# Squares of the output projection issued as tasks, and the last 256 tokens written token by token

## The chip, the cores and the metric

The kernel runs on one core of one Trainium2 chip. The metric is the device time of one execution in microseconds (us); the number of a kernel is the median of its runs.

## The reference

The program is one step of a two-layer network (DEPTH 2, width D_MODEL 2048) on 128 context tokens and 512 latent tokens, 640 in all. Each layer normalises its input, runs two mixers beside each other (attention and gated linear attention in layer 0, neighbourhood attention and a gated MLP in layer 1), multiplies by a gate and projects back to 2048 features. The change touches only what surrounds the two projections back and the final norm:

```python
def rms_norm(x, g, eps=1e-6):
    xf = x.astype(jnp.float32)
    y = xf * lax.rsqrt(jnp.mean(xf * xf, axis=-1, keepdims=True) + eps)
    return (y * g.astype(jnp.float32)).astype(x.dtype)
...
for l in range(DEPTH):
    shift, scale, gate = modulation(c_ctx, ada_w[l], ada_b[l])
    h = rms_norm(x, norm_g[l]) * (1.0 + scale) + shift
    ...
    x = x + gate * (y @ w_out[l])
y_prompt = rms_norm(x, final_norm_g)
```

For the latent tokens the same is done with their own modulation. So after each projection the squares of x have to be summed over the 2048 features of each token, once for the norm of layer 1 and once for the final norm.

## The kernel before

**Layout.** Activations lie with features on the 128 partitions and tokens along the free axis: a strip is 128 features by 640 tokens, and 16 strips make a token's 2048 features. Context tokens are columns 0 to 127, latent tokens 128 to 639.

**Products.** Weights and activations are single precision, each split into a high and a low part: `whi` and `wlo` for weights, `acth` and `actl` for activations. One product is three matrix instructions: `acth` by `whi`, `actl` by `whi`, `acth` by `wlo` (all at line 397). ACT makes a high part by copying into the shorter format; POOL makes a weight's low part by subtracting it (`wlo<-wraw,whi`, or `wlo<-rs,whi` for sums of two weight tiles, in line 214, through which every ACT, DVE and POOL instruction passes). So ahead of each group of products there is a weight load on SP, a row of ACT and a row of POOL.

**Order.** There is no order by hand. A planner in the program (`Pace`) keeps a model of when each engine will be free. The products set its time; between them `tick` calls issue weight splits (`wpump`) and give a turn to tasks, which are Python generators put on a list with `spawn`. A task goes on when the flags that it names are set (`wait`), when the model says that its operand is ready (`until`) and when the engines that it names are not booked further ahead than so many us (`calm`). A step that the main program needs can be forced with `need`, which gives turns to the tasks until the flag is there. What is issued on one engine is run in that order. All DMAs that this text speaks of go out on SP's queue (`dma`, line 431), but for the last transfers, of which every other one goes out on ACT's (line 2684).

**The projections back.** `out_proj(l)` runs over 16 output strips, for layer 1 in the order of their features, for layer 0 in the order OUT0. The first two are computed together by `kpair`, the next twelve two by two by `spair`, which shares sums of weight tiles (a scheme of Strassen's kind), and the last two by `kpair` in layer 0 and by `hpair` in layer 1. `hpair` computes columns 0 to 383 (CUT) of both strips first and then columns 384 to 639, so that the first part can be finished while the second is computed. `spair` overwrites halves of `acth` and `actl`; the kept copies lie in DRAM (`bh_dram`, `bl_dram`) and `unfold` (line 1130) brings them back for the last pair, one copy at each turn of the task.

**Evacuation.** `out_evac` (line 1969) makes, for each strip, a function that takes the product out of its bank: y = G·product + x, on DVE, into one of eight slots of Y (NY = 8). In the same call it has the squares summed: `ssq_add` (line 1240) lets ACT write y² into a buffer and POOL add it to `ssq`:

```python
        def square(y, c):
            if l == 1 and f == KT - 1:
                nc.scalar.activation(self.sq[:, : c.stop - c.start], y[:, c], AF.Square)
            else:
                self.ssq_add(self.ssq, y, f, self.sq if self.cut == CUT else self.sqs.next(), c)
```

For the first fourteen strips this happens in two halves of 320 columns; in the profile these rows are `arena<-Y 128x320` on ACT and `arena<-arena 128x320` on POOL. The buffers are a ring of two (`sqs`). The last two strips of layer 0 had their squares in a task of their own (`squares`) already. The strips of y go to DRAM too (`spill`): in layer 1 the first eight, since Y has only eight slots, and `reload` (line 2638) fetches them again when the copies of `unfold` are in, into free parts of rs, arena and adas. `handover` with its task `rewrite` (line 994) turns the strips of layer 0 into the `acth` and `actl` of layer 1.

**The end.** `final(half)` (line 2646) runs twice, for columns 0 to 383 and 384 to 639. A product with a matrix of ones sums `ssq` over the partitions, so that every partition holds the sum of each token; `rms` makes the root of its inverse by Ln and Exp on ACT and one step of Newton's on DVE, on rows as wide as the half. Then each of 16 strips is multiplied by the final gain g (a value for each partition) and by the token's root (a row), on DVE, or on POOL for the five strips of POOLED, where ACT has multiplied by g ahead of time. Two strips go out with each DMA, as runs of 1.5 KB in the first half and 1 KB in the second.

Of the kernel before, what the change touches and what calls it, by code (L numbers as in the profile page):

```python
# [14 lines left out]
ALU = mybir.AluOpType  # L15
# [224 lines left out]
class Trunk:  # L240
# [601 lines left out]

    def hpair(self, c1, c2, after):

        self.cut = CUT
        for half, order in enumerate(((AGAIN, KEPT), (KEPT, AGAIN))):
            if half:
                self.quiet, self.hold = True, 6.0
            p = {}
            for end in range(2):  # L850
                for c in (c1, c2):
                    if not end:
                        if half == 0 and self.chunks[c][3]:
# [140 lines left out]
    def handover(self, ready, free, used, order, at, src, loads, spare, cs, shift=None):  # L994
# [26 lines left out]

        def rewrite():
            if shift is not None:
                yield from self.wait("shift1")
            for k in order:
                yield from self.wait(f"{free}:{k}", f"in:{k}", *(f"evac{c}" for c in cs if k in (6, 7)))
                x = tile_(k)
                yield from self.until(x)
                while (w := self.pace.ready("a", [self.pace.span(x)], []) - self.now) > 0:
                    yield w  # L1030
                yield from self.calm(self.calms[0], "ag")
                if shift is not None:
# [12 lines left out]
                yield  # L1045
# [923 lines left out]
    def out_evac(self, l, n, f, xsrc, spill):  # L1969
        nc = self.nc  # L1970
        box = {}

        def square(y, c):
            if l == 1 and f == KT - 1:
                nc.scalar.activation(self.sq[:, : c.stop - c.start], y[:, c], AF.Square)
            else:
                self.ssq_add(self.ssq, y, f, self.sq if self.cut == CUT else self.sqs.next(), c)

        def squares(y):
            if n == KT - 1:  # L1980
                yield from self.wait("squares")
            for q, s in ((slice(0, HT), self.sqs.next()), (slice(HT, T), self.sqs.next())):
                yield from self.wait("x1:14")
                yield from self.calm(2.0, "a")
                nc.scalar.activation(s, y[:, q], AF.Square)
                yield from self.until(s)
                yield from self.calm(4.0, "v")
                nc.vector.tensor_tensor(self.ssq[:, q], self.ssq[:, q], s, ALU.add)
                yield
            self.flags.add("squares")  # L1990

        def evac(pa, pb):
            G, at = self.G[l], self.cut
            y = self.Y[:, n % NY, :]
            if pa is not None:
                if n < NY:
                    self.clear(f"Y{n}", "C", "R")
                x = box["x"]
# [25 lines left out]
        return pre, evac  # L2024
# [144 lines left out]
    def program(self):  # L2169
# [473 lines left out]
        self.flags.add("reload")  # L2643
        yield

    def final(self, half):
        nc, d, L = self.nc, self.d, self.L
        c = slice(CUT, T) if half else slice(0, CUT)
        n = c.stop - c.start
        t, u = (m[:, :n] for m in L["ms"])  # L2650
        if half:
            yield from self.wait("prescaled")
        p = self.sm()[:, :n]
# [3 lines left out]
        yield from self.until(self.sq[:, :n])  # L2657
        self.mm(p, self.ones, self.sq[:, :n], start=False)
        if not half:
            yield 0.8  # L2660
        self.rms(r, p, t)
        q = self.sm()[:, :n]
        nc.vector.scalar_tensor_tensor(q, t, 1.5, r, ALU.add, ALU.mult)
        if half:
            nc.scalar.activation(u, t, AF.Copy, bias=1.5)
            nc.gpsimd.tensor_tensor(u, u, r, ALU.mult)
            self.flush()
        else:
            nc.scalar.activation(u, q, AF.Copy)
            self.flags.add("fr")  # L2670
            yield from self.wait("reload")
        at = 0
        for k in range(KT):
            y, g = self.x2(k)[:, 0, c], self.fg[:, k : k + 1]
            if k in self.POOLED:
                if not half:
                    yield from self.calm(1.5, "a")
                    nc.scalar.activation(self.x2(k), self.x2(k), AF.Copy, scale=g)
# [3 lines left out]
            if half and (k % 2 or k == 0):  # L2682
                eng = (nc.sync, self.tc.nc.scalar)[(k + 1) // 2 % 2]
                eng.dma_start(d["o_y"][:, at : k + 1, c], self.x2(at, k + 1 - at)[:, :, c])
                at = k + 1
            elif k % 2 and not half:
                self.dma(d["o_y"][:, k - 1 : k + 1, c], self.x2(k - 1, 2)[:, :, c])
            if not half:
                if k == self.POOLED[-1]:
                    self.flags.add("prescaled")  # L2690
                yield 0.3
        self.flags.add(f"final{half}")
        yield


class Ring:
# [9 lines left out]


_OUTS = {
    "o_y": [128, KT, T],
    "o_ak": [2, 128, 128],  # L2710
    "o_av": [2, 128, 128],
    "o_state": [2, 4, 128, 256],
# [109 lines left out]


def _result(r):
    y = r["o_y"].transpose(2, 1, 0).reshape(T, D)
# [32 lines left out]
```

## Time and profile before

| | before |
|---|---|
| median of 3 runs | 2104.3 us (2100.51, 2104.3, 2105.4) |
| profiled execution, whole | 2104.64 us |
| its span, first to last instruction | 2102.8 us |
| mean granted TensorE clock | 0.996 |
| busy: TensorE | 98% |
| busy: DVE / ACT / POOL | 62% / 51% / 62% |
| bytes moved | 340.18 MB |

A row of a timeline reads: start, duration, engine, line, operation, output<-inputs, shapes, count, and in brackets how long the engine stood idle before it and what ended that. A row of groups reads: line, engine, operation, names and shapes, count | busy us, mean ns of one | idle time before them and what ended most of it. A row of a window reads: stretch, its length, busy us (instructions) of PE, PEld, DVE, ACT and POOL, then the granted TensorE clock, the busy share of the DMA engines and GB/s. PE is TensorE, PEld its weight loads, SPq the queue of SP. Line numbers are those of the kernel before.

### The profile page before, as it was taken

Reading aid. Unit: us, or ns where it says so; the run is one execution under the profiler, and the core shown is the slowest. Engines: PE = TensorE matmul, PEld = TensorE weight load, DVE = VectorE, ACT = ScalarE, POOL = GpSimd, SP = SyncE. Lnnn points to the kernel's source line nnn. Section 1 sums busy time; section 2 is a strip of 40 time slices with the busy share of each in tenths; the row PEclk is TensorE's granted clock in tenths of the full one; section 3 lists DMA queues with packets and bytes.
Section 4 is the critical chain, followed back from the end, with each engine's and each line's share of the span. In section 5 each row is a group of like instructions: output and inputs, shape, how many; then the busy total and the mean of one; then the engine's idle time right before and its main releaser. Section 6 shows DMA issues by size and latency. Waiting matters only on the chain.

```text
span 2102.8 us, 40256 instructions
## 1 busy us (share of the span) xinstructions
PE 2052.0 (98%) x14345; PEld 2000.7 (95%) x14345; DVE 1305.9 (62%) x3034; ACT 1078.3 (51%) x2485; POOL 1301.4 (62%) x1090
## 2 busy tenths in 40 slices
PE   7999999999999999999999999999999999999997
PEld 6899999999999999999999999999999999999996
DVE  4746586676465664787376878787454444466434
ACT  5645565554566866543564434444444544454443
POOL 4656565355455563888755656555655577767884
PEclk9999999999999999999999999999999999999998
DMA  9966343335465544565634454444222344363426
GB/s 362 389 218 207 120 140 123 116 116 175 149 200 173 171 162 149 175 211 181 227 126 129 131 167 152 137 149 148 97 75 94 105 134 131 120 224 116 139 93 240
DMA packets 192841, 340.18 MB, mean 162 GB/s; under 512 B 20896, under 2 KB 70144, under 8 KB 192640
## 3 DMA queue, kind: packets, MB, share of 16 engines
q1 hardware_dynamic: 191296, 336.45, 48.4%
q8 instruction: 112, 1.84, 0.4%
q10 hardware_dynamic: 1344, 1.17, 0.2%
q14 instruction: 89, 0.73, 0.1%
HBM read 303.03 MB, written 31.88 MB: 159 GB/s over the span
## 4 chain that ended last, share of the span: by engine, by line
PE 79%; DMA 7%; DVE 6%; POOL 3%; issue 3%; ACT 2%; SPq 1%; ACTq 0%; POOLq 0%; DVEq 0%
PE bank L397 76%; POOL wlo L214 2%; PE bank L402 2%; DVE arena L214 1%; DVE adas L214 1%; DVE Y L214 1%; DMA adas<-gateT 1%; DMA more<-ada 1%; DVE bank L214 1%; ACT arena L214 1%; DMA Y<-xT 1%; DMA adas<-ada 1%; SPq L431 1%; PE bank L1426 1%; POOL actl L214 0%
## 5 line engine op out<-in xcount | busy, mean ns | idle before, releaser
L397 PE MATMUL bank<-acth,whi 128*128 128x320 f32 (+3 forms) x3320 | 1020.9, 318 | 7.3 <-ACT bc L214 3.0
L397 PE MATMUL bank<-acth,wlo 128*128 128x320 f32 (+3 forms) x3320 | 993.9, 310 | 3.2 <-POOL wlo L214 3.0
L397 PE MATMUL bank<-actl,whi 128*128 128x320 f32 (+3 forms) x3320 | 993.2, 310 | 1.1 <-DMA actl<-bl_dram 1.1
L214 POOL TENSOR_TENSOR wlo<-wraw,whi 128x512 fp32r<-128x512 f32 (+1 forms) x446 | 564.5, 1278 | 388.9 <-ACT whi L214 302.3
L397 PEld LDWEIGHTS bank<-acth,whi 128*128 128x128 f32 (+1 forms) x3320 | 617.1, 189 | 16.2 <-ACT bc L214 4.4
L397 PEld LDWEIGHTS bank<-acth,wlo 128*128 128x128 f32 (+1 forms) x3320 | 617.2, 189 | 4.7 <-POOL wlo L214 4.7
L397 PEld LDWEIGHTS bank<-actl,whi 128*128 128x128 f32 (+1 forms) x3320 | 617.2, 189 | 3.2 <-DMA actl<-bl_dram 1.6
L214 POOL TENSOR_TENSOR wlo<-rs,whi 128x384 fp32r<-128x384 f32 x370 | 409.2, 1125 | 190.8 <-ACT whi L214 154.3
L214 ACT ACTIVATE whi<-wraw 128x512 fp32r<-128x512 f32 (+1 forms) x456 | 260.7, 587 | 93.0 <-PE bank L397 66.4
L214 ACT ACTIVATE whi<-rs 128x384 fp32r<-128x384 f32 x370 | 183.3, 517 | 59.4 <-PE bank L397 51.2
L397 PE MATMUL bank<-eh,wlo 128*128 128x322 f32 (+1 forms) x666 | 206.8, 311 | 2.2 <-POOL wlo L214 2.2
L397 PE MATMUL bank<-eh,whi 128*128 128x322 f32 (+1 forms) x666 | 209.0, 314 | 0.0
L397 PE MATMUL bank<-el,whi 128*128 128x322 f32 (+1 forms) x666 | 206.8, 310 | 0.0
L214 DVE TENSOR_TENSOR wraw<-rs 128x768 f32<-128x768 f32 x74 | 99.1, 1339 | 131.6 <-DMA rs<-w_odd 46.6
L214 POOL TENSOR_TENSOR prod<-adas,mixrow 128x512 f32<-128x512 f32 x94 | 123.6, 1324 | 84.4 <-ACT prod L214 59.1
L214 DVE CUSTOM_DVE_ANT_0 adas<-adas,bank,partg 128x256 bf16<-128x256 f32 (+1 forms) x290 | 156.2, 539 | 12.0 <-DMA adas<-ada_g 4.6
L214 ACT ACTIVATE arena<-arena,bc 128x512 f32<-128x512 f32 (+4 forms) x189 | 97.8, 538 | 76.4 <-DVE arena L214 71.3
L397 PEld LDWEIGHTS bank<-eh,wlo 128*128 128x128 f32 x666 | 125.5, 188 | 3.5 <-POOL wlo L214 3.5
L397 PEld LDWEIGHTS bank<-el,whi 128*128 128x128 f32 x666 | 125.8, 189 | 0.0
L397 PEld LDWEIGHTS bank<-eh,whi 128*128 128x128 f32 x666 | 125.5, 188 | 0.1
L214 DVE TENSOR_TENSOR bank<-bank,sums 128x320 f32<-128x320 f32 (+1 forms) x148 | 70.7, 493 | 72.8 <-PE bank L397 56.3
L214 DVE CUSTOM_DVE_ANT_0 adas<-adas,bank,part 128x512 bf16<-128x512 f32 x142 | 105.6, 744 | 9.5 <-DMA adas<-ada 6.9
(221 smaller groups left out, 2467.7 us busy)
## 6 DMA issues: line engine op xcount, KB each, us to landing
wraw<-w_even SPq DMA_DIRECT2D x176, 256.0 KB, 3.4
adas<-ada_g SPq DMA_DIRECT2D x128, 256.0 KB, 3.6
adas<-ada SPq DMA_DIRECT2D x128, 256.0 KB, 3.6
rs<-w_odd SPq DMA_DIRECT2D x50, 384.0 KB, 3.2
wraw<-w_odd SPq DMA_DIRECT2D x74, 256.0 KB, 3.6
wraw<-w_out SPq DMA_DIRECT2D x60, 256.0 KB, 3.5
rs<-w_odd SPq DMA_DIRECT2D x50, 256.0 KB, 3.9
Y<-ada SPq DMA_DIRECT2D x24, 512.0 KB, 7.7
```

What stands on the lines that cost most here:

```text
L214: return f(*args, **kw)
L397: self.nc.tensor.matmul(out, lhsT, rhs, start=start, stop=stop, **kw)
L402: self.nc.tensor.transpose(out, in_, self.ident[:k, :k])
L431: self.nc.sync.dma_start(out, in_)
L1426: nc.tensor.matmul(o, c, w, start=j < 4, stop=j >= 12)
```

## The change

Three things are changed.

1. *Squares.* For the first fourteen strips of both projections `square` no longer issues anything; it spawns a task `late` for each half. The task waits for the task before it, for y, until ACT is booked no more than 1.0 us ahead for the square, and until POOL is booked no more than 1.5 us ahead for the addition, and then sets a flag `sq{l}:{i}`. Three places now ask for such a flag: an evacuation of strip 8 and later (the squares of the strip whose slot it overwrites), the evacuations of the last pair in layer 1, and `rewrite`.
2. *Final gain ahead of time.* `prescale` and `scale` multiply columns 384 to 639 of each strip by g in place, on whichever of ACT, DVE and POOL the planner holds free first; the last two strips get it in a row of DVE behind their evacuation (`ends2`).
3. *The last 256 tokens.* `final` now does columns 0 to 383 only. `last` does the rest with tokens on the partitions: 32 transposes of 128x128 by TensorE bring the scaled strips into eight banks, six products with two columns of ones sum the squares for each token into one column, the root is made on 4 columns, and each bank is copied out to SBUF by ACT or DVE in turn with the root as a value for each partition. Eight transfers on SP write them to a new output `o_z` [256 tokens, 2048], six of them in runs of 2 KB. The host puts both outputs together.

```diff
@@ hpair @@
-        self.cut = CUT
+        self.cut, self.ends2 = CUT, []
...
-            self.spawn(after(half), first=True)
+            self.hb = list(p.values())
+            self.spawn(after() if half else self.final(), first=True)
@@ handover, rewrite @@
-                yield from self.wait("shift1")
+                yield from self.wait("shift1", f"sq0:{2 * KT - 5}")
@@ out_evac @@
         def square(y, c):
-            if l == 1 and f == KT - 1:
+            if n < KT - 2:
+                self.spawn(late(y, c, 2 * n + (c.start > 0)))
+            elif l == 1 and f == KT - 1:
                 nc.scalar.activation(self.sq[:, : c.stop - c.start], y[:, c], AF.Square)
+            elif l == 1 and f == KT - 2 and c.start == CUT:
+                nc.scalar.activation(self.sqs.list[0][:, : T - CUT], y[:, c], AF.Square)
...
+        def late(y, c, i):
+            yield from self.wait("ssq" if i == 0 else f"sq{l}:{i - 1}")
+            yield from self.until(y[:, c])
+            yield from self.calm(1.0, "a")
+            if i < 2:
+                nc.scalar.activation(self.ssq[:, c], y[:, c], AF.Square)
+            else:
+                s = self.sqs.next()
+                nc.scalar.activation(s, y[:, c], AF.Square)
+                yield from self.until(s)
+                yield from self.calm(1.5, "g")
+                nc.gpsimd.tensor_tensor(self.ssq[:, c], self.ssq[:, c], s, ALU.add)
+            self.flags.add(f"sq{l}:{i}")
+            yield
...
+            if at == CUT:
+                self.need(f"sq1:{2 * KT - 5}")
...
+                else:
+                    self.need(f"sq{l}:{2 * (n - NY) + 1}")
...
+                if at == CUT:
+                    nc.vector.tensor_scalar(x[:, at:T], y[:, at:T], self.fg[:, f : f + 1], None, ALU.mult)
+                    self.ends2.append(x[:, at:T])
@@ program @@
-        do(lambda: self.spawn(self.reload()))
+        do(lambda: [self.spawn(x) for x in (self.reload(), self.prescale())])
-        pair("h", self.final)
+        pair("h", self.last)
@@ new: scale, prescale, last @@
+    def scale(self, k):
...
+        if e == "a":
+            nc.scalar.activation(x, x, AF.Copy, scale=g)
+        else:
+            (nc.vector if e == "v" else nc.gpsimd).tensor_scalar(x, x, g, None, ALU.mult)
...
+    def last(self):
...
+        def put(g):
+            for j in range(4):
+                x = rows[4 * (g // 2) + j][:, 128 * (g % 2) : 128 * (g % 2) + 128]
+                self.tr(bank[g][:, 128 * j : 128 * j + 128], x)
...
+        for i in range(2):
+            for j, x in enumerate(parts):
+                self.mm(p[:, 2 * i : 2 * i + 2], x[:, 128 * i : 128 * i + 128], self.ones[:, 0:2], start=j == 0, stop=j == 2)
...
+        self.rms(r, p, t)
+        nc.vector.scalar_tensor_tensor(r, t, 1.5, r, ALU.add, ALU.mult)
+        put(6)
+        for g, (b, o) in enumerate(zip(bank, outs)):
+            if g == 5:
+                yield from self.wait("final0")
+                put(7)
...
+            if i:
+                nc.vector.tensor_scalar(o, x, r[:, 2 * i : 2 * i + 1], None, ALU.mult)
+            else:
+                nc.scalar.activation(o, x, AF.Copy, scale=r[:, 2 * i : 2 * i + 1])
+            z = d["o_z"][128 * i : 128 * i + 128, 512 * k : 512 * k + 512]
+            nc.sync.dma_start(z if len(o.shape) == 2 else z.rearrange("p (a b) -> p a b", b=T - CUT), o)
```

How this moves instructions is seen in the order of each engine. First POOL, behind the evacuation of the first pair of strips in layer 1's projection, as it was before (`wlo` are low parts of weights, `arena<-arena` an addition of squares):

```order
L214 TENSOR_TENSOR wlo<-rs_8159,whi 128x384
L214 TENSOR_TENSOR arena_8164<-arena_8164 128x320 x2
L214 TENSOR_TENSOR wlo<-rs_8159,whi 128x384
L214 TENSOR_TENSOR wlo<-wraw,whi 128x384 x2
L214 TENSOR_TENSOR wlo<-rs_8159,whi 128x384 x2
L214 TENSOR_TENSOR arena_8164<-arena_8164 128x320
L214 TENSOR_TENSOR wlo<-rs_8159,whi 128x384 x2
```

The same place of POOL now:

```order
L214 TENSOR_TENSOR wlo<-rs_8159,whi 128x384 x2
L214 TENSOR_TENSOR wlo<-wraw,whi 128x384 x2
L214 TENSOR_TENSOR wlo<-rs_8159,whi 128x384 x4
L214 TENSOR_TENSOR wlo<-wraw,whi 128x512
L214 TENSOR_TENSOR wlo<-wraw,whi 128x384 x2
L214 TENSOR_TENSOR wlo<-rs_8159,whi 128x384 x3
L214 TENSOR_TENSOR arena_8164<-arena_8164 128x320
```

The three additions that stood between these low parts come behind them.

Then SP's queue in the last pair of layer 1, before (`acth<-bh_dram` and `actl<-bl_dram` are the copies of `unfold`, `wraw<-w_out` are weight loads):

```order
L431 DMA wraw<-w_out 128x512
L431 DMA acth<-bh_dram 128x320
L431 DMA wraw<-w_out 128x512
L431 DMA actl<-bl_dram 128x320
L431 DMA acth<-bh_dram 128x320
L431 DMA wraw<-w_out 128x512
L431 DMA actl<-bl_dram 128x320
L431 DMA wraw<-w_out 128x512
```

and now:

```order
L431 DMA wraw<-w_out 128x512
L431 DMA actl<-bl_dram 128x320
L431 DMA acth<-bh_dram 128x320
L431 DMA wraw<-w_out 128x512
L431 DMA actl<-bl_dram 128x320
L431 DMA acth<-bh_dram 128x320
L431 DMA wraw<-w_out 128x512
L431 DMA actl<-bl_dram 128x320
```

The last copy stood ahead of the last load of this piece and now stands behind it.

Last, TensorE behind its last product of weights. Before, only a sum by ones followed it:

```order
L397 MATMUL bank_68<-acth,whi 128x256
L397 MATMUL bank_68<-actl,whi 128x256
L397 MATMUL bank_68<-acth,wlo 128x256
L397 MATMUL bank_73<-arena_8164,ones 128x256 x2
```

Now (the six products with 128x2 are the sums for each token, `ident` marks transposes):

```order
L397 MATMUL bank_69<-acth,wlo 128x256
L402 MATMUL bank_67<-ident,rs_8159 128x128 x4
L402 MATMUL bank_68<-ident,rs_8159 128x128 x4
L402 MATMUL bank_70<-ident,arena_8164 128x128 x2
L402 MATMUL bank_70<-ident,adas 128x128 x2
L397 MATMUL bank_74<-ones,arena_8164 128x2 x6
L402 MATMUL bank_73<-ident,arena_8164 128x128 x2
L402 MATMUL bank_73<-ident,adas 128x128 x2
L402 MATMUL bank_71<-ident,Y 128x128 x4
L402 MATMUL bank_69<-ident,Y 128x128 x4
```

Three banks are filled ahead of the sums and the others behind them; two more banks follow with the same kinds of rows.

More of the change, by code (lines that the diff above doesn't have):

```diff
@@ L2644, in reload, with prescale, final @@
         yield
-    def final(self, half):
-        nc, d, L = self.nc, self.d, self.L
[L2648 to L2653, printed above, removed]
+    def scale(self, k):
+        if k >= KT - 2 or f"sc{k}" in self.flags:
+            return
+        nc, t = self.nc, self.pace.t
+        x, g = self.x2(k)[:, 0, CUT:T], self.fg[:, k : k + 1]
+        yield from self.until(x)
+        while f"sc{k}" not in self.flags:
+            w, e = min((max(t[e], self.now) + w, e) for e, w in (("a", 0.4), ("v", 0.4), ("g", 0.8)))
+            if w < self.now + 1.5:
+                break
+            yield w - self.now - 1.4
+        else:
+            return
+        if e == "a":
+            nc.scalar.activation(x, x, AF.Copy, scale=g)
+        else:
+            (nc.vector if e == "v" else nc.gpsimd).tensor_scalar(x, x, g, None, ALU.mult)
+        self.flags.add(f"sc{k}")
+    def prescale(self):
+        yield from self.wait(f"sq1:{2 * KT - 5}")
+        for k in (*range(NY, KT - 2), *range(NY)):
+            if k == 0:
+                yield from self.wait("reload")
+            yield from self.scale(k)
+            yield
+        self.flags.add("scaled")
+        yield
+    def final(self):
+        nc, d, L = self.nc, self.d, self.L
+        c = slice(0, CUT)
+        t, u = (m[:, :CUT] for m in L["ms"])
+        p = self.sm()[:, :CUT]
         r = self.rstd[:, c]
@@ L2656, in final @@
         self.mm(p, self.ones, self.ssq[:, c], stop=False)
[L2657 to L2660, printed above, removed]
+        yield from self.until(self.sq)
+        self.mm(p, self.ones, self.sq, start=False)
+        yield 0.8
         self.rms(r, p, t)
-        q = self.sm()[:, :n]
+        self.qb = self.sm()
+        q = self.qb[:, :CUT]
         nc.vector.scalar_tensor_tensor(q, t, 1.5, r, ALU.add, ALU.mult)
[L2664 to L2672, printed above, removed]
+        nc.scalar.activation(u, q, AF.Copy)
+        yield from self.wait("reload")
         for k in range(KT):
             y, g = self.x2(k)[:, 0, c], self.fg[:, k : k + 1]
+            yield from self.scale(k)
             if k in self.POOLED:
-                if not half:
-                    yield from self.calm(1.5, "a")
-                    nc.scalar.activation(self.x2(k), self.x2(k), AF.Copy, scale=g)
+                yield from self.calm(1.5, "a")
+                nc.scalar.activation(y, y, AF.Copy, scale=g)
                 nc.gpsimd.tensor_tensor(y, y, u, ALU.mult)
@@ L2681, in final @@
                 nc.vector.scalar_tensor_tensor(y, y, g, q, ALU.mult, ALU.mult)
[L2682 to L2691, printed above, removed]
@@ L2708 @@
 _OUTS = {
-    "o_y": [128, KT, T],
+    "o_y": [128, KT, CUT],
+    "o_z": [T - CUT, D],
     "o_ak": [2, 128, 128],
@@ L2824, in _result @@
 def _result(r):
-    y = r["o_y"].transpose(2, 1, 0).reshape(T, D)
+    y = np.concatenate([r["o_y"].transpose(2, 1, 0).reshape(CUT, D), r["o_z"]], 0)
     heads = lambda t: np.ascontiguousarray(t.transpose(2, 0, 1))[None, None]
```

32 lines of the change are left out of this document (31 added, 1 removed).

## The prediction

> **What bounds the kernel now.** I read the page first, then who waited for whom, then the timeline at the waits and behind the last matrix product. From the page:
>
> ```profile
> span 2102.8 us, 40256 instructions
> PE 2052.0 (98%) x14345; PEld 2000.7 (95%) x14345; DVE 1305.9 (62%) x3034; ACT 1078.3 (51%) x2485; POOL 1301.4 (62%) x1090
> ```
>
> TensorE is busy for 98% of the span, and the change takes nothing off its products. So it can gain only where TensorE waits, and behind its last product. The list of TensorE's waits, for the whole run and then for 870 to 980, 1890 to 1930 and 2040 to 2080 us (total, times, longest):
>
> ```profile
> PE bank L397 <- POOL wlo L214: 5.2, 7, 1.1
> PE bank L397 <- POOL wlo L214: 3.7, 5, 1.0
> PE bank L397 <- POOL wlo L214: 1.1, 1, 1.1
> PE bank L397 <- DMA actl<-bl_dram: 1.1, 2, 0.6
> ```
>
> Six of the seven waits for a weight's low part (wlo) lie in the first strips of the two output projections, 3.7 us in layer 0 and 1.1 us in layer 1: 4.8 us. The seventh (0.4 us, the rest of 5.2) is in the last pair. What holds POOL there is shown by the timeline at 955 to 972 us and at 1914 us (the last row is a window behind them, with the busy time of PE, PEld, DVE, ACT and POOL):
>
> ```profile
> 960.69 0.99 ACT L214 ACTIVATE arena<-Y 128x320 f32<-128x320 f32 x2 [6.07 <-DVE Y L214]
> 961.24 2.44 POOL L214 TENSOR_TENSOR arena<-arena 128x320 f32<-128x320 f32 x2 [4.76 <-ACT arena L214]
> 963.64 2.68 POOL L214 TENSOR_TENSOR wlo<-wraw,whi 128x384 fp32r<-128x384 f32 x2
> 1914.72 1.02 POOL L214 TENSOR_TENSOR arena<-arena 128x320 f32<-128x320 f32 x1 [0.89 <-ACT arena L214]
> ...
> 1920.00:1940.00 20.00, 20.00 (x138) 20.00 (x137) 9.22 (x13) 8.84 (x20) 18.57 (x17) 1.00 0.47 156
> ```
>
> ACT stands 6.07 us before a square (arena<-Y) because its operand Y is not there; POOL stands 4.76 us before the addition of that square. Each engine takes its instructions in order, so the low parts that TensorE waits for stand behind them. The engines are not full; the order holds them.
>
> Behind the last product (it starts at 2087.51 and lasts 0.28) come 15.0 us. The first window shows the DMA engines nearly empty, the next ones full:
>
> ```profile
> 2087.51 0.28 PE L397 MATMUL bank<-acth,wlo 128*128 128x256 f32 x1
> ...
> 2088.00:2090.00 2.00, 1.40 (x4) 0.59 (x4) 1.36 (x3) 1.93 (x5) 2.00 (x3) 1.00 0.17 62
> 2090.00:2093.00 3.00, 0.00 (x0) 0.00 (x0) 2.09 (x5) 1.16 (x3) 1.67 (x3) 0.85 1.00 360
> 2093.00:2095.00 2.00, 0.00 (x0) 0.00 (x0) 2.00 (x6) 0.00 (x0) 1.92 (x4) 0.50 0.61 211
> 2095.00:2100.00 5.00, 0.00 (x0) 0.00 (x0) 2.20 (x6) 0.00 (x0) 1.63 (x3) 0.50 1.03 341
> 2101.00:2102.80 1.80, 0.00 (x0) 0.00 (x0) 0.00 (x0) 0.00 (x0) 0.00 (x0) 0.50 0.15 54
> ...
> 2084.59 0.37 SPq L431 DMA_DIRECT2D o_y<-arena  x1
> 2089.15 2.28 SPq L431 DMA_DIRECT2D o_y<-Y  x3
> 2097.47 1.09 SPq L431 DMA_DIRECT2D o_y<-Y  x1
> ```
>
> (The last two numbers of a window are the DMA engines' busy share and GB/s; SPq rows are SP issuing a transfer, 0.37 us at its quickest and 0.76 in the crowded three.) Between 2090 and 2101.3 the engines are at their limit except for 0.8 us of room at 2093 to 2095. The tail is a chain of instructions up to about 2092 and a queue of bytes after it.
>
> **The change, part by part.**
>
> *Squares as tasks.* The same number of squares and additions, so no engine gains or loses work; what moves is their place. In the new order of POOL in layer 1 the three additions that stood ahead of the strip's low parts come after all of them, so that wait goes: 1.1 us. In layer 0 the low parts of the sum (wlo<-wraw) pass two additions of 2.44 us together, more than the longest wait of 1.0 us there; the later ones still have one square or two between them. Bounds: all 4.8 us go, or none (POOL's additions of 1.0 us each land ahead of a later low part that is just as urgent). I take 3.0 of 3.7 us in layer 0, since the freed place is longer than each wait, and all of layer 1: **-4.1 us**. The new waits of the evacuation for squares of eight strips ago and of the rewriting for the last square of layer 0 only order the program; the squares they name stand ahead of them by then, and I cost them at nothing. Their cover is the eight strips in between and, for the rewriting, the last pair of strips; with it gone the price is one late addition, 1.0 us.
>
> *The fetch of the kept halves.* In the last pair each copy back (acth<-bh, actl<-bl) now stands behind one more weight load on SP. The last of them decides:
>
> ```profile
> 2065.40 0.32 SPq L431 DMA_DIRECT2D actl<-bl_dram  x1
> 2065.90 0.33 SPq L431 DMA_DIRECT2D wraw<-w_out  x1
> ...
> 2069.61 0.45 PE L397 MATMUL bank<-actl,whi 128*128 128x384 f32 x1 [0.64 <-DMA actl<-bl_dram]
> ```
>
> The two change places. The load waits for a slot (it went at 2065.90), so the copy goes at about 2066.0 in place of 2065.40, lands 0.6 us later, and TensorE has that wait on top. From its issue to the product that waited for it went 4.2 us (2069.61 less 2065.40). Bounds: 0, if it travels less crowded there, and 1.1, if the copies come to cost TensorE twice what they cost it now. I take most of the delay of the issue: **+0.5 us.**
>
> *The scaling by the final gain ahead of time.* Fourteen strips of 128x256 on ACT, DVE and POOL, most of them while POOL has nothing to do:
>
> ```profile
> 2082.61 1.02 POOL L214 TENSOR_TENSOR rs<-rs,arena 128x384 f32<-128x384 f32 x1 [9.88 <-ACT rs L214]
> L214 POOL TENSOR_TENSOR Y<-Y,arena 128x256 f32<-128x256 f32 x3 | 2.1, 727 | 0.0
> ```
>
> Six on POOL at 0.73 us (two operands; one operand is not shown at this size) are 4.4 us in 9.9 us of idle time; even at double that they fit. One more scaling on ACT comes before the table load, some 0.4 us on the first 384 tokens, which are not last. Nothing on the path; without that cover 4.4 us.
>
> *The tail.* It removes eleven DVE rows and five POOL rows of 256 tokens and the row-wide root; it adds 32 transposes, six small products, a root on 4 columns and eight evictions of 128x512.
>
> ```profile
> L402 PE MATMUL bank<-ident,Y 128*128 128x128 f32 x108 | 20.6, 273 | 0.5 <-DVE Y L214 0.5
> L397 PE MATMUL bank<-small,adas 128*128 128x2 f32 x48 | 7.7, 230 | 3.9 <-ACT adas L214 3.0 <-DVE adas L214 0.9
> L214 ACT ACTIVATE bc<-bank 128x2 f32<-128x2 f32 x90 | 15.3, 170 | 155.3 <-DVE arena L214 148.8 <-DVE YB L214 4.4 <-DVE Y L214 1.4
> L214 ACT ACTIVATE Y<-bank 128x512 f32<-128x512 f32 x37 | 22.1, 598 | 52.4 <-PE bank L397 41.5 <-PE bank L402 10.3
> L214 DVE TENSOR_SCALAR arena<-bank 128x320 f32<-128x320 f32 x8 | 3.9, 492 | 5.0 <-PE bank L397 4.8
> L214 DVE SCALAR_TENSOR_TENSOR Y<-Y,small,bank 128x384 f32<-128x384 f32 x5 | 2.9, 604 | 0.0
> L214 DVE SCALAR_TENSOR_TENSOR el<-part,eh 128x4 fp32r<-128x4 f32 x2 | 0.2, 158 | 0.0
> ```
>
> From the last product's end, 2087.8, on DVE: the last evacuation to 2088.3 (0.5), one scaling to 2088.6, the four rows of the first 384 tokens that stand ahead (4 x 0.60) to 2091.0. TensorE needs 12 x 0.19 = 2.3 us for transposes (20.6 over 108) and 6 x 0.16 = 1.0 us for the sums, to 2091.1, beside it. ACT's two small rows at 0.17 end at 2091.4 and DVE's three at 2091.9. Then ACT evicts four banks at 0.60 and DVE four at 0.79 (0.49 for 320 columns, and 512 at the same pace), the last at 2095.1. SP issues eight transfers from 2092.5 on; at 0.37 us each it is ruled by the evictions and ends at 2095.5, at 0.76 it ends at 2098.6, where the last issue ended before. By instructions alone the tail is up to 3.1 us shorter.
>
> By bytes it is not. After the first pair of strips (0.39 MB, in the empty time before 2090.5) there remain 3 x 0.39 + 8 x 0.26 = 3.28 MB, and the first of these start only when POOL has done its rows, near 2091.2. At 360 GB/s (1.5 KB runs, row 2090 to 2093) that is 9.1 us, so 2100.3 against 2101.3; at 341 (1 KB runs) 9.6 us. Six of the eight new transfers have runs of 2 KB; I take 365. **-1.2 us**, bounds +1.0 (a hole like that at 2093, and late rows) and -3.0.
>
> [...]
>
> Against the change speaks that DVE's scalings read and write SBUF while POOL runs:
>
> ```profile
> L214 DVE TENSOR_SCALAR Y<-Y,A 128x512 f32<-128x512 f32 x3 | 1.4, 478 | 0.0
> L214 DVE TENSOR_SCALAR adas<-adas,A 128x128 f32<-128x128 f32 x1 | 1.6, 1635 | 0.0
> ```
>
> A quarter of the elements took over three times as long beside POOL, a loss of some 1.4 us (1.64 less a quarter of a microsecond). The one scaling behind the last evacuation could be held that long: DVE's small rows end at 2092.9 and the first transfer goes at 2093.5, still before the strips ahead of it have left (2091.2 + 1.18 MB at 360 = 2094.5). So it costs nothing as long as the queue of bytes is there. [...]
>
> **The sum.** -4.1 + 0.5 - 1.2 = -4.8 us. The span of 2102.8 becomes 2098.0. That execution took 2104.6 (1.8 us around the span), 0.3 over the median of 2104.3, so I forecast 2104.3 - 4.8 = **2099.5 us**.
>
> **The rivals.**
>
> *The squares only change the victim.* POOL is busy for 62% on the page, but for 18.57 of 20 us in the strips of layer 1 that follow (1920 to 1940); there a later low part may wait as long. For it: the same additions stand between low parts of the next strip. Against: no wait is seen in those strips now. Then 0.5 - 1.2: 2103.6.
>
> *The tail is ruled by instructions.* If the strips of the first half leave sooner than I have it and the new runs go faster, -3.0 with the rest as forecast: 2097.7. Against it the share of 1.03.
>
> *Slower: the copies back.* On SP every copy now waits with the load ahead of it, for a slot that a low part must free. If the last copy falls among the reload's large copies, it takes what this one took:
>
> ```profile
> adas<-yT_dram SPq DMA_DIRECT2D x1, 640.0 KB, 9.6
> ```
>
> Issued at 2066.0 and landing 9.6 us later it is there at 2075.6, 6.0 us after 2069.6. With the squares changing only the victim and the tail giving 1.2, that is 2104.3 + 6.0 - 1.2 = 2109.1. It decides from a landing of about 4 us past 2069.6 on. For it: the small copy already took 4.2 us. Against: the large ones are still issued behind it.
>
> **How the numbers follow.** Forecast 0.50, victims changed 0.22, instruction-ruled tail 0.14, copies back 0.14. What a measurement here can tell from no change is about 0.2%, 4.2 us: faster means below 2100.1, slower above 2108.5. The forecast's own range is 2097.5 to 2102, of which a bit under two thirds lies below 2100.1: 0.32, and with the shorter tail 0.46. Slower are two thirds of the copies' case, 0.10, the rest of it landing a little earlier. Within: what remains, 0.44. For 8 in 10: below, all 4.8 us with the short tail and no loss are 2096.5; above, no gain from the squares, none in the tail and 0.5 lost are 2104.8; and since three runs of one kernel lie 4.9 us apart, their median may lie a third of that, 1.6 us, to either side: 2094.9 to 2106.4. Beyond lies little but the copies' case.
>
> **What would show it.** Right: no wait of TensorE for POOL's wlo at the first strips of both projections, additions of squares behind wlo rows, the last product some 3.6 us earlier; then the DMA share near 1 from the first o_z to the end, and 14 us behind the last product. Wrong: waits for wlo of 1 us in later strips; a wait for actl<-bl_dram of over 2.2 us; a tail of 12 us (bytes do not rule) or over 15 (the small root or the evictions are late).

## The result, and the profile after

The changed kernel takes 2107.03 us (median of 20 runs, 2101.35 to 2110.78), the kernel before 2103.15 (20 runs beside them, 2100.51 to 2106.22). The ratio is 1.0017, with an interval of 1.0010 to 1.0024: slower by some 3.9 us, where 4.8 us faster was forecast. The profiled execution took 2107.09 us.

From the page after:

```profile
span 2105.3 us, 40368 instructions
PE 2058.5 (98%) x14385; PEld 2007.0 (95%) x14385; DVE 1307.0 (62%) x3028; ACT 1086.0 (52%) x2497; POOL 1294.6 (61%) x1089
```

The shares tell nothing, since they are those of before. What tells is where time was lost. The 11,958 products with a weight's part (line 397) are the same in number and order in every kernel of this study, so the start of the same product can be compared in two traces. The starts of products 4180, 5540, 5610, 10600, 11825 and 11957 (the last), counted from 0, cut each trace into stages; in the profile of before they lie at 845.8, 1053.0, 1063.3, 1882.5, 2066.1 and 2087.5 us. The first row gives the length of each stage before, the others what is added to it (us, one profile each):

| kernel | to the 1st projection | 1st projection | hand-over to layer 1 | layer 1 | 2nd projection | last pair | last product to end |
|---|---|---|---|---|---|---|---|
| before | 845.80 | 207.23 | 10.31 | 819.20 | 183.57 | 21.40 | 15.32 |
| the change | -3.71 | -1.72 | **+4.45** | +0.96 | -0.19 | **+2.51** | +0.17 |
| squares alone | -4.25 | -3.29 | +3.29 | -0.15 | -0.29 | +0.15 | -0.01 |
| end alone | -4.93 | +0.65 | 0.00 | +0.64 | +0.03 | +2.14 | +0.49 |
| change, strip mended | -1.62 | -1.83 | 0.00 | +0.77 | -0.21 | +1.05 | +0.17 |
| change, copies mended | +4.62 | -2.49 | +2.86 | +0.94 | -0.19 | +0.23 | +0.17 |
| squares, strip mended | -0.45 | -3.43 | 0.00 | +0.03 | -0.28 | +2.31 | -0.01 |
| squares, both mended | -3.74 | -2.65 | 0.00 | +0.59 | -0.27 | -0.67 | -0.02 |
| change, both mended | -1.97 | -1.81 | 0.00 | +0.74 | -0.18 | -0.74 | +0.21 |
| the same, no scaling | -4.61 | -2.60 | 0.00 | +0.77 | -0.19 | -1.05 | -1.07 |
| both mended, scaling on POOL | -3.93 | -2.15 | 0.00 | +1.29 | -0.18 | -0.75 | -1.20 |
| before, copies mended | -0.22 | -0.21 | 0.00 | +0.04 | -0.07 | -1.34 | -0.06 |

The first stage runs the same instructions in all twelve and lies between 840.9 and 850.4 us. That is the scatter of single runs, and the reason why one span against another says little here, while the later stages repeat to some tenths, or mostly show a cause where they don't. The scatter goes with the granted clock: where it fell to half once in this stage, for 3.41 us, the stage took 840.9 to 842.1 us (five profiles, the change among them), with two falls 842.1 to 845.8 (six, the kernel before among them), with four 850.4 (experiment 4).

**The hand-over.** The list of TensorE's waits in the changed kernel, for 1045 to 1064 us:

```profile
PE bank L397 <- POOL wlo L214: 1.2, 1, 1.2
PE bank L397 <- ACT whi L214: 1.1, 1, 1.1
```

Before there was no wait here at all. What made the first parts of the weights late stands some 15 us earlier, in the timelines of ACT, SP and DVE. Before:

```profile
1034.86 1.13 DVE L214 SCALAR_TENSOR_TENSOR Y<-bank,G,arena 128x128 f32<-128x128 f32 x3
1036.02 0.32 SPq L431 DMA_DIRECT2D x1T_dram<-Y  x1
1039.07 1.00 ACT L214 ACTIVATE Y<-Y,A 128x128 f32<-128x128 f32 x2
1041.27 1.00 ACT L214 ACTIVATE Y<-Y,A 128x128 f32<-128x128 f32 x2
```

After:

```profile
1029.45 1.13 DVE L214 SCALAR_TENSOR_TENSOR Y<-bank,G,arena 128x128 f32<-128x128 f32 x3
1033.32 0.38 SPq L431 DMA_DIRECT2D x1T_dram<-Y  x1
1034.36 1.00 ACT L214 ACTIVATE Y<-Y,A 128x128 f32<-128x128 f32 x2
1039.88 1.02 ACT L214 ACTIVATE Y<-Y,A 128x128 f32<-128x128 f32 x2 [3.74 <-DMA x1T_dram<-Y]
1053.24 0.61 ACT L214 ACTIVATE whi<-wraw 128x512 fp32r<-128x512 f32 x1
```

And the rows of this transfer among the DMA issues (KB and us from issue to landing), before and after:

```profile
x1T_dram<-Y SPq DMA_DIRECT2D x1, 320.0 KB, 3.2
```

```profile
x1T_dram<-Y SPq DMA_DIRECT2D x1, 320.0 KB, 6.5
```

ACT rewrites the strips in place (Y<-Y,A), and the second strip is the one that was evacuated last and is still being read on its way to DRAM. Before, that transfer went out 0.03 us behind the evacuation (1036.02 against 1034.86 + 1.13) and landed at 1039.2, 2.1 us before ACT came to the strip. Now it goes out 2.7 us behind (1033.32 against 1030.58), behind seven transfers that have passed it and into DMA engines that are full (share 1.01 from 1033.32 to 1039.82 us), takes 6.5 us in place of 3.2 and lands at 1039.8. ACT stands for 3.74 us, and all that is behind it on ACT moves, to the high part at 1053.24, for which TensorE waits 1.1 us. The order of SP there, before (left) and now (right):

```
wraw<-w_out                       | wraw<-w_out
acth<-bh_dram                     | acth<-bh_dram
x1T_dram<-Y     (the strip)       | arena<-xT
arena<-xT                         | arena<-x1T_dram
arena<-x1T_dram                   | actl<-bl_dram
actl<-bl_dram                     | arena<-xT
arena<-xT                         | wraw<-w_out
arena<-x1T_dram                   | arena<-x1T_dram
acth<-bh_dram                     | acth<-bh_dram
adas<-x1T_dram                    | x1T_dram<-Y     (the strip)
```

**The last pair.** The timeline of TensorE in the changed kernel, and then three windows of 3.41 us (columns as before, the granted clock third from the end):

```profile
2068.16 0.44 PE L397 MATMUL bank<-actl,whi 128*128 128x384 f32 x1 [0.66 <-DMA actl<-bl_dram]
2070.15 0.59 PE L397 MATMUL bank<-actl,whi 128*128 128x384 f32 x1 [1.12 <-DMA actl<-bl_dram]
```

```profile
2066.88:2070.29 3.41, 1.64 (x8) 0.89 (x7) 0.00 (x0) 0.00 (x0) 0.78 (x1) 1.00 1.04 361
2070.29:2073.70 3.41, 3.41 (x11) 3.41 (x12) 0.74 (x2) 0.52 (x1) 1.16 (x2) 0.50 1.01 383
2073.70:2077.11 3.41, 3.41 (x23) 3.41 (x23) 0.53 (x2) 0.00 (x0) 3.41 (x4) 1.00 0.51 204
```

The waits are the two of before, 1.8 us in place of 1.1. But for the 3.41 us behind them TensorE ran at half its clock: 11 products lie in that window, 23 in the next. The same stands at the hand-over:

```profile
1053.12:1056.53 3.41, 1.38 (x7) 1.11 (x8) 2.50 (x6) 3.38 (x8) 3.04 (x3) 1.00 0.00 0
1056.53:1059.94 3.41, 3.41 (x15) 3.41 (x14) 2.58 (x7) 1.75 (x5) 2.75 (x2) 0.50 0.43 126
1059.94:1063.36 3.42, 3.42 (x25) 3.42 (x24) 2.67 (x7) 2.82 (x6) 2.19 (x2) 1.00 0.84 264
```

So the 4.45 us of the hand-over are the holes in TensorE's row and 10 products less than the 25 of a full window, some 1.4 us.

**The end.** Three windows of 2 us from the last product on, first of before and then of the change:

```profile
2087.51:2089.51 2.00, 1.37 (x7) 0.67 (x5) 1.53 (x3) 2.00 (x4) 2.00 (x3) 1.00 0.41 152
2089.51:2091.51 2.00, 0.31 (x2) 0.00 (x0) 0.67 (x2) 1.17 (x3) 1.52 (x2) 1.00 0.74 267
2091.51:2093.51 2.00, 0.00 (x0) 0.00 (x0) 1.93 (x6) 0.42 (x1) 1.07 (x2) 0.64 0.90 323
```

```profile
2089.81:2091.81 2.00, 2.00 (x21) 2.00 (x20) 1.97 (x5) 1.05 (x3) 0.92 (x2) 1.00 0.76 273
2091.81:2093.81 2.00, 2.00 (x20) 1.96 (x19) 1.92 (x4) 0.85 (x3) 1.90 (x2) 1.00 0.59 212
2093.81:2095.81 2.00, 1.29 (x10) 0.85 (x8) 1.90 (x5) 1.57 (x3) 0.00 (x0) 1.00 0.59 210
```

The DMA engines have room (share 0.59) between 2 and 6 us behind the last product, because the strips of the first 384 tokens are not ready: DVE is full (1.9 of 2 us). What is missing there has to be moved later; experiments 8 and 9 test what holds it up.

### The profile page after: what moved, and what is told of

It reads as the page before. It is cut to its first block, busy times and chain, and to the rows that moved or that the text cites. A ratio compares the mean times of both kernels' runs of the same rounds, so it can differ in the third digit from the quotient of the medians.

```text
span 2105.3 us, 40368 instructions
## 1 busy us (share of the span) xinstructions
PE 2058.5 (98%) x14385; PEld 2007.0 (95%) x14385; DVE 1307.0 (62%) x3028; ACT 1086.0 (52%) x2497; POOL 1294.6 (61%) x1089
```

## The experiments

All times are medians of 7 to 12 runs beside runs of the kernel before on the same chip (2103.15 us in the first four, 2102.90 in the next four, 2102.09 in the last two).

**1. Squares alone.** The kernel before with the tasks `late` and the waits for their flags, and with its old end.

> The squares as tasks alone, with the old end of the kernel. Theory A (the loss sits where the deferred squares let transfers change places on SP: the last strip of layer 0 goes to DRAM later, and ACT waits for it before it rewrites that strip): the profile shows the same wait of ACT for x1T_dram<-Y of 3 to 4 us near 1036, TensorE without weights for 2 to 3 us near 1053 and a granted clock of 0.5 behind it, 4.5 us in all, and 2 us gained in the projections; so 2 to 4 us slower than before. Theory B (the new end of the kernel, with its scalings and transposes, is the loss): 2 us faster than before, no such wait.

Measured: 2102.74 us, ratio 1.0003 (0.9994 to 1.0012). The wait is there, in the timeline of ACT; behind it two windows of 3.41 us:

```profile
1038.07 1.02 ACT L214 ACTIVATE Y<-Y,A 128x128 f32<-128x128 f32 x2 [4.08 <-DMA x1T_dram<-Y]
```

```profile
1049.71:1053.13 3.42, 1.81 (x11) 1.27 (x9) 3.42 (x10) 2.77 (x6) 1.52 (x2) 1.00 0.00 0
1053.13:1056.54 3.41, 2.33 (x16) 2.33 (x17) 1.66 (x4) 2.36 (x5) 3.33 (x3) 1.00 0.22 74
```

The hand-over costs 3.29 us, and theory A has its place right. But the clock did not fall in this run: the hole lies over two windows of 3.41 us, with 11 and 16 products in them. The projections give more than I expected (3.6 us), so the kernel as a whole is not slower.

**2. The end alone.** The changed kernel with the squares issued in the evacuation as before.

> The scaling ahead of time and the end token by token alone, squares issued in the evacuation as before. Theory A: no wait of ACT at the hand-over, the first strips of the projections as before, and from the last product to the end 15.3 to 15.6 us as before; within 1 us of before. Theory B: 3 to 4 us slower than before.

Measured: 2105.14 us, ratio 1.0007 (0.9996 to 1.0017). No wait at the hand-over; 15.8 us from the last product to the end. The last pair is 2.14 us longer, though its transfers stand in the order of before there: the waits for the copies were 1.5 us and the clock fell to 0.50 behind them. So neither theory had all of it: that stage depends on something that the order does not tell.

**3. The strip mended.** In the evacuation, behind the transfer of the strip:

```diff
                     self.dma(spill[:, f, :], y)
+                    self.pace.due([self.pace.span(y)])
```

`due` issues, in their order, all transfers put off up to the last one that touches y.

> The changed kernel with one line more: the transfer of a strip of y to DRAM is issued at its evacuation, ahead of transfers that are planned behind it. Theory A: the wait of ACT for x1T_dram<-Y goes from 3.7 us to under 0.5, TensorE's 2.4 us of waits near 1053 and the 0.5 clock behind them go, 4 to 4.5 us faster than the changed kernel and some 0.5 us faster than before; the copies at the end still cost. Theory C (the deferred squares hold ACT and POOL ahead of the first weights of layer 1, whatever the transfer does): within 1 us of the changed kernel.

Measured: 2101.37 us, ratio to before 0.9997 (0.9988 to 1.0007). At the hand-over TensorE waits for nothing, the stage is 10.31 us as before, and the rows are these, of the timeline and of the DMA issues:

```profile
1032.60 0.32 SPq L431 DMA_DIRECT2D x1T_dram<-Y  x1
1036.34 1.00 ACT L214 ACTIVATE Y<-Y,A 128x128 f32<-128x128 f32 x2
1038.02 1.00 ACT L214 ACTIVATE Y<-Y,A 128x128 f32<-128x128 f32 x2
```

```profile
x1T_dram<-Y SPq DMA_DIRECT2D x1, 320.0 KB, 3.0
```

One line takes the whole loss away; theory C falls. The medians differ by 5.7 us (2107.03 less 2101.37), the stage by 4.45; the rest is within the scatter of the other stages.

**4. The copies mended.** The loads of raw weights are held while the last two pairs of copies are issued (`holdw`; the condition keeps it to layer 1):

```diff
-        while self.nraw < len(self.plain) and self.job > self.wneed[self.nraw]:
+        while not self.holdw and self.nraw < len(self.plain) and self.job > self.wneed[self.nraw]:
...
         for i, j in enumerate(JT):
+            self.holdw = i >= 4 and "sq1:10" in self.flags
...
+        self.holdw = False
         self.flags.add("unfold")
```

> The changed kernel with two loads of weights in the last pair moved on SP behind the last copies of kept halves. Theory A: TensorE's waits for actl<-bl_dram near 2068 to 2070 go from 1.8 us to under 1.0, the granted clock stays at 1.00 there instead of 0.57 for 4 us, and the last product comes 2 to 3 us earlier; the hand-over still costs 4.5. Rival: the moved loads are then late, and TensorE waits for wlo instead, 1 us or more, and nothing is gained.

Measured: 2105.19 us, ratio 1.0008 (0.9998 to 1.0017). One wait of 0.8 us is left, the clock stays at 1.00, and the stage is 2.3 us shorter than in the change (+0.23 against +2.51). The moved loads are not late. The hand-over costs 2.86 us again, with a wait of ACT of 3.63 us. TensorE's waits there are 2.3 us as in the change (1.3 and 1.0), but the clock stayed at 1.00; so some 1.6 of the change's 4.45 us came with the fall.

**5. Squares alone, strip mended.** Experiment 1 with the line of experiment 3.

> The squares as tasks with the old end, and the strip's transfer issued at its evacuation. Theory A: no loss at the hand-over, the gain of the projections stays (1.7 to 3.3 us in layer 0, 0.3 in layer 1): 2 to 3.5 us faster than before, 2099.5 to 2101. Rival: the gain in the projection was only the earlier place of rows that are then missing at the hand-over, and with the transfer in its old place the gain goes too: within 1 us of before.

Measured: 2099.02 us, ratio 0.9985 (0.9976 to 0.9994): 3.9 us faster than before. The first projection keeps its gain (-3.43) and the hand-over costs nothing. The gain is one of its own and not lent by the hand-over. In this profile the last pair cost 2.31 us:

```profile
2062.76:2066.17 3.41, 1.99 (x8) 0.97 (x6) 0.00 (x0) 0.00 (x0) 1.72 (x3) 1.00 0.96 309
2066.17:2069.58 3.41, 3.23 (x10) 3.23 (x11) 0.74 (x2) 0.52 (x1) 0.75 (x1) 0.50 0.99 369
```

**6. Squares alone, both mended.**

> The same with two weight loads moved behind the last copies. If the waits for the copies are a steady cost, 0.5 to 1 us faster than the kernel without that move; if they cost much only when the granted clock falls behind them, which a single run shows or not, the same within 1 us, with no fall of the clock in its profile.

Measured: 2097.39 us (2096.05 to 2098.19), ratio 0.9971 (0.9960 to 0.9981). TensorE waits for no copy, and the stage is 0.67 us shorter than before. It is 1.6 us faster than experiment 5, so what the move saves lies above the 0.5 to 1 us of a steady wait; the clock does not fall in its last pair (1.00 in every window of 2 us from 2060 to 2072 us). It is the fastest kernel here, and its runs lie closest together.

**7. The whole change, both mended.**

> The whole change with both mends, the new end included. Theory A: every stall that the change brought is gone, so what is left is the new end alone: from the last product to the end 15.3 to 15.5 us, as before, and the kernel as fast as the one with the old end and both mends, within 1 us. Rival (the new end costs outside its own stage, by its scalings in the last pair): 1 to 2 us slower than that one.

Measured: 2101.33 us, ratio 0.9986 (0.9976 to 0.9996). From the last product to the end 15.53 us. It is 3.9 us slower than experiment 6, more than the rival had: its profile shows 0.2 us for the end and some 0.7 us in layer 1 (see the sum below), so the rest of that difference isn't settled.

**8. No scaling.** As 7, without the sixteen multiplications by the final gain, so that the last 256 tokens lack that factor.

> As the one before, but the last 256 tokens are not multiplied by the final gain: the sixteen scalings are left out. Theory A for the end (the scalings hold back the rows of the first 384 tokens on DVE, ACT and POOL, and the DMA engines stand partly empty between 2 and 6 us behind the last product): from the last product to the end 1 to 2 us shorter, 13.5 to 14.5 us. Rival (the bytes alone rule): 15.3 to 15.5 us, no change.

Measured: 2098.48 us, ratio 0.9978 (0.9967 to 0.9989). From the last product to the end 14.25 us, 1.3 us shorter than in 7, where theory A had it. The scalings are the price of the new end.

**9. Scaling on POOL.** As 7, but the strips that come back from DRAM are scaled right there, in the task that fetches them:

```diff
             self.dma(self.x2(k, 2), self.ysp[:, k : k + 2, :])
             yield
+        for k in range(NY):
+            x = self.x2(k)[:, 0, CUT:T]
+            self.nc.gpsimd.tensor_scalar(x, x, self.fg[:, k : k + 1], None, ALU.mult)
+            self.flags.add(f"sc{k}")
```

> The whole change with both mends, and the eight strips that come back from DRAM scaled by POOL as soon as they are there, instead of by whichever engine the planner holds free. If the scalings on ACT and DVE in the last 4 us before the end of the products are what the new end pays for, then from the last product to the end some 1 us less (14.2 to 14.8 us) and the kernel 0.5 to 1.5 us faster than with the mends alone, about as fast as the one with the old end; if POOL's rows hold up a low part instead, TensorE waits for wlo near 2084 by as much and nothing is gained.

Measured: 2098.70 us (2096.88 to 2100.06), ratio 0.9980 (0.9971 to 0.9989), 2.6 us faster than 7, or 1.8 us when each is set against the kernel before that ran beside it (3.4 and 1.6 us faster). From the last product to the end 14.12 us. The timeline of POOL and two windows from 2 us behind the last product on:

```profile
2066.79 3.66 POOL L214 TENSOR_SCALAR rs<-rs,small 128x256 f32<-128x256 f32 x4
2071.55 2.06 POOL L214 TENSOR_SCALAR arena<-arena,small 128x256 f32<-128x256 f32 x2 [1.10 <-DMA arena<-yT_dram]
2073.59 1.82 POOL L214 TENSOR_SCALAR adas<-adas,small 128x256 f32<-128x256 f32 x2
```

```profile
2083.79:2085.79 2.00, 2.00 (x20) 2.00 (x20) 1.85 (x6) 0.47 (x2) 0.84 (x1) 1.00 1.00 360
2085.79:2087.79 2.00, 1.07 (x10) 0.83 (x8) 1.97 (x4) 1.86 (x4) 0.00 (x0) 1.00 0.80 284
```

With the scalings in POOL's idle time the DMA share there is 1.00 and 0.80 in place of 0.59 and 0.59 (in the 2 us ahead of these windows it is 0.56 in place of 0.76). TensorE's wait for a low part in the last pair is 0.6 us, as in 7, so the rows on POOL add none.

**10. Before, copies mended.** The kernel before with only the held loads of experiment 4.

> The kernel before with only this: the weight loads of the last pair go out behind the last copies of kept halves. If the copies are a cost that the kernel before pays too, its 1.1 us of waits there go and it is 0.7 us faster, more in the runs in which the clock falls behind such a wait; if they were a cost of the change alone, no difference.

Measured: 2101.01 us, ratio 0.9988 (0.9980 to 0.9997), 1.1 us faster. The waits for the copies are a cost that the kernel before pays too; they are not the change's.

## Why the prediction was wrong, point by point

**The view of the bound** was right: TensorE's waits and the end are where nearly all of the time was won and lost. Some 0.7 us in layer 1 lie in neither (see the sum).

**Squares, -4.1.** The mechanism holds: low parts no longer stand behind additions that wait. The size was off. The two projections give 1.9 us in the change's profile, and 1.9 to 3.7 in the nine kernels with the squares as tasks. I had the waits of layer 0 go from 3.7 us to 0.7; 1.3 are left in the changed kernel's list, for 860 to 1040 us:

```profile
PE bank L397 <- POOL wlo L214: 0.5, 1, 0.5
PE bank L397 <- DVE Y L214: 0.5, 1, 0.5
PE bank L397 <- ACT whi L214: 0.3, 1, 0.3
```

Two of them are new, for ACT and DVE: with POOL's waits shorter, the next late engine shows. In layer 1 half of the 1.1 us stays.

**The delayed squares at the hand-over, costed at nothing,** are the step that failed. I wrote that the new waits "only order the program", with the strips in between as cover and a late addition, 1.0 us, as the price without it. The stage came out 4.45 us longer. The flag is not what cost it: in experiment 3 the rewriting still asks for it, and the stage is 10.31 us as before. The rewriting waited for the transfer of the strip that it overwrites, for which the sum had no term. The planner puts a transfer off until its operand is ready, but issues it at once when an instruction is recorded that touches the same data (`record` calls `due`); in the kernel before that instruction was the square. So a square that comes later takes with it the early place of a transfer on SP. I followed the squares on ACT and POOL and quoted SP's order only in the last pair; that the row x1T_dram<-Y now stands behind seven more was to be seen in the same order, at the hand-over. Experiment 3 shows it: 3.0 us for the transfer instead of 6.5, and +4.45 us go to 0.00. The tasks alone bring the loss (3.29 us in experiment 1), the end alone doesn't.

**The kept halves, +0.5.** The waits grew by 0.7 us (1.1 to 1.8), close to that. What I didn't have is the 3.41 us at half clock behind them, which make it 2.51. And that the new order is the reason is not shown: experiment 1 has that order and lost 0.15, experiment 2 has the old one and lost 2.14. The kernel before waits for copies there already (1.1 us), and experiment 10 takes 1.1 us from its time. With the unmended copies the clock fell to 0.50 there in the change and in experiments 2 and 5, and stayed at 1.00 in experiments 1 and 3 and in the kernel before; what decides it is open.

**Scaling ahead of time: "nothing on the path".** Wrong. I looked for the cover on POOL and it was there (9.9 us), and six of the fourteen went there, at 0.92 us each. But the planner put the last ones where there is none: on ACT and DVE, among the rows of the first 384 tokens. In the changed kernel:

```profile
2086.16 0.50 ACT L214 ACTIVATE arena<-arena,small 128x256 f32<-128x256 f32 x1
2086.56 1.00 ACT L214 ACTIVATE adas<-adas,small 128x256 f32<-128x256 f32 x2
2088.93 0.35 DVE L214 TENSOR_SCALAR adas<-adas,small 128x256 f32<-128x256 f32 x1
```

Leaving all of it out gives 1.28 us (experiment 8), moving it to POOL 1.41 (experiment 9).

**The end, -1.2.** Measured +0.17 in the change and -1.20 in experiment 9. The small root was not late: its last row ends 4.4 us behind the start of the last product, as forecast (2091.9 less 2087.51; here 2094.20 less 2089.81):

```profile
2094.04 0.16 DVE L214 SCALAR_TENSOR_TENSOR last<-last,last 128x4 f32<-128x4 f32 x1
```

So the forecast size comes once the scalings are out of the way; in the change the rows that feed the DMA engines were late, on the side of the bound of +1.0 that I gave for that. Some slips of the sum change nothing: by its own figures the bytes end at 2100.2 and give -1.1, and SP's quickest issue in the rows that it shows is 0.32 us, not 0.37.

**The rivals.** The slower one had its place in the last pair, by copies that take 9.6 us. That place did lose time, by another mechanism, but the larger loss lay where I had no rival. The victims of the squares did change in part (ACT and DVE in the list above).

**What the sum comes to.** In the change's own profile, -1.72 - 0.19 + 4.45 + 2.51 + 0.17 + 0.96 = +6.2 us behind the first stage, which itself was 3.7 us shorter by chance (one fall of the clock there in place of two): 2.5 us in the span. The medians say 3.9. For layer 1 the sum had no term. All seven kernels with the new end lose 0.6 to 1.3 us there, and against the kernel before they do it at the same places: 0.20, 0.23 and 0.07 us over the second, third and fourth 500 products of that stage, to 0.01 us in each of the seven, and under 0.01 us in the four with the old end. In experiment 2, where the order of layer 1 is that of before, the 0.64 us are made of steps of no more than 0.01 us. So the new end costs some 0.7 us there; why is open. The 0.59 us of experiment 6 is another matter, nearly all of it one step of 0.55 us, which the change and experiment 9 have too and for which no cause is shown.

## What to carry to other kernels

When an instruction is moved, ask what its place did for others: here a read of the data forced a transfer out early, and the read was moved alone. Where a program puts transfers off until they are due, read the order of the DMA queue at each later overwriting of what they carry, not only where the change speaks of transfers. Before work is called free because an engine is idle, look where the scheduler really puts it, and compare traces stage by stage from a common instruction: whole runs scatter by more than the effects looked for (the 20 of the kernel before over 5.7 us).

## What was not expected of the hardware

Ahead of the last product TensorE's granted clock fell to half 25 times in the twelve profiles, each time for 3.41 us, and within a run at distances of whole steps of 3.41 us (in the kernel before at 61.15 and 115.76 us, 16 steps of 3.413 us apart; in the change at 49.60, 1056.53 and 2070.29 us, 295 and 297 such steps apart). In the later stages each of the four falls followed a window of that length in which TensorE stood for much of the time: it was busy for 1.38 and 1.64 us in the change's two windows shown, for 1.95 in experiment 2 and 1.99 in experiment 5. With 1.81 and 2.33 us at the hand-over of experiment 1 it stayed at 1.00. So a hole in TensorE's row cost here up to 1.7 us more (an estimate, half of the 3.41), or nothing more. What decides is not shown, but neither the busy time nor the number of TensorE's instructions does it alone. In experiment 6 a window with 38 instructions, 1.81 us, was followed by a fall, and one with 11, 1.52 us, was not (each with the window behind it):

```profile
99.07:102.48 3.41, 1.81 (x38) 1.61 (x38) 3.27 (x10) 1.73 (x5) 2.19 (x3) 1.00 1.04 402
102.48:105.90 3.42, 3.42 (x40) 2.92 (x39) 1.92 (x6) 1.44 (x5) 3.30 (x3) 0.50 0.97 367
174.17:177.59 3.42, 1.52 (x11) 1.26 (x9) 1.85 (x6) 1.13 (x3) 3.39 (x3) 1.00 0.90 208
177.59:181.00 3.41, 2.65 (x18) 2.65 (x19) 1.45 (x4) 3.35 (x9) 0.35 (x1) 1.00 0.80 255
```

The strip's transfer of 320 KB, which took 3.2 us from issue to landing before and 3.0 in experiment 3, took 6.5 in the change, where seven others had passed it and the DMA share was 1.01.
